# Raising weight splits, bank-emptying instructions and state updates in the order of ScalarE and VectorE

## The chip, the cores and the metric

The kernel runs on one core of a Trainium2 chip. The metric is device time in microseconds (us) of one execution; lower is better. The core has a matrix engine (TensorE, rows PE, its weight loads PEld), VectorE (DVE), ScalarE (ACT), GpSimd (POOL) and SyncE (SP), which here only issues DMA transfers. TensorE writes its results into PSUM banks, and a bank can be written anew only when VectorE or ScalarE has read it out.

## The reference, cut to what matters

One layer of a hybrid decoder: 512 prompt tokens and 64 sample tokens (8 sequences of 8) are normalised, one wide projection feeds three branches, and the branches are gated, summed and projected back. All is float32. The change touches the second branch, a Mamba-2 state-space branch (SSD) with 8 groups of 4 heads, computed in chunks of 128 tokens:

```python
xbc, conv_new = _causal_conv(xbc, conv0, conv_w, conv_b)      # 4 taps, then silu
xs, bm, cm = jnp.split(xbc, [D_INNER, D_INNER + SSD_GROUPS * SSD_STATE], axis=-1)
dt = jax.nn.softplus(dt_raw + dt_bias)
...
cb = jnp.einsum('bclgn,bcsgn->bgcls', cc, bc)
y_diag = jnp.einsum('bgcls,bgrcls,bcsgrp->bclgrp', cb, decay, xc)
states = jnp.einsum('bcsgn,bgrcs,bcsgrp->cbgrpn', bc, decay_states, xc)
h_final, h_prev = lax.scan(step, h_init, (states, chunk_decay))   # h * d + s
y_off = jnp.einsum('bclgn,cbgrpn,bgrcl->bclgrp', cc, h_prev, jnp.exp(a_cs))
...
y = y_diag + y_off + xh * d_skip[:, None]
h_b = _gated_group_rmsnorm(y.reshape(bsz, L, D_INNER), z, ssd_norm_g)   # y * silu(z), normed by group
m = g_a * (h_a @ w_proj_a) + g_b * (h_b @ w_proj_b) + g_x * (h_x @ w_proj_x)
```

## The kernel before, in words

The SSD branch is the first large stage, from about 40 to 637 us. Tokens lie along the free axis (512 + 64 = 576 columns), channels on the 128 partitions. A projection of 128 output channels is a **job** of two halves of 288 columns. Its weights come by DMA as `wraw` (two buffers, each for two jobs). `prep` splits one job's 128x1024 weights into a rounded high part `whi`, a cast on ScalarE, and a low part `wlo`, a subtraction on VectorE (both in `split`, lines 98 and 99; two buffers each). `half(f)` issues 24 matmuls (8 slices of the contraction times whi·xhi, whi·xlo, wlo·xhi, line 167) into one of three `acc` banks, and then the instructions that empty that bank.

There are four kinds of jobs. `conv_job` (four for each group) empties its bank into `raw` (lines 404, 408, 409, ScalarE) and, after the second half, runs the convolution: one scaled copy on ScalarE (line 416), three taps on VectorE (line 418), a tanh on ScalarE (line 420) and a product on VectorE (422, 426, 429); its results are `xs` and `C`. `z_job` (two for each group) empties with a tanh (462) and a product (463) into `zs`. `proj_job` multiplies the normed groups `hb` by the output projection and adds the bank to `m_sb` (753, 755). `gate_job` (eight, late) takes a tanh (732).

Between the halves stand the **steps** of the current group: transposes of a chunk (503) into an `sps` bank, from which `xdt`, `xdd` and `BT` are made (506, 509, 511); the product C·B (532) multiplied into the decays `e` (533); the diagonal part (548) added to `ysb` (559); the state matmul (567) and the state update `hT` (571, 573, 574); the off-diagonal part (592, 595, 597); for the samples the state `h` (653, 658, 659) and the stacked operands `xv`, `xst`, `bst`, `btd` (622 to 631). `gate_y` and `norm_y` norm the group before: a product, a square, two matmuls with a matrix of ones (699, 700), Ln and Exp on ScalarE (701, 702), a product (705), and a split into `hb` (again lines 98 and 99). There are three `sps` and two `yps` banks.

The order of TensorE is fixed by hand: `units` lists halves and steps, and inside `tc.manual_schedule` TensorE issues in the order in which the code emits. ScalarE and VectorE are ordered by a scheduler at build time: among the instructions that it takes to be ready, an engine gets the one with the lowest number, and the number is the place in the order of emission (TensorE's instructions count too). The result is one fixed queue for each engine; on the chip an engine takes its queue in that order and waits where an operand or a buffer isn't there. In the last loop below, the weights of job i+1 are split when the first half of job i is issued, and the loads of job i+2 are issued at the same place:

```python
i = at[id(j)]
if h == 0:
    if i + 2 < len(jobs):
        jobs[i + 2].load()
    if i + 1 < len(jobs):
        jobs[i + 1].prep()
j.half(h)
```

Of the kernel before, what the change touches and what calls it, by code (L numbers as in the profile page):

```python
# [42 lines left out]
def tile_hybrid_step(  # L43
# [33 lines left out]
    def s_tile():  # L77
# [12 lines left out]
                     compare_op=ALU.is_ge, fill=0.0, base=LS - 1, channel_multiplier=-1)  # L90


    lo_last = [False]
# [106 lines left out]
    with ExitStack() as stb:  # L200
# [177 lines left out]
        def conv_job(g, ci):  # L378
# [14 lines left out]
            def half(f):  # L393
                ps, _ = gemm_half(k["w"], KD, xh, xl, f)
                if f == 0:
                    if ci == 0:
                        d["xs"] = pb.tile([P, 3, TW], F32, tag="xs", name="xs", bufs=2)
                        d["C"] = pb.tile([P, T], F32, tag="C", name="C", bufs=2)
                        d["cg"] = pb.tile([P, 4, 27], F32, tag="cg", name="cg", bufs=2)
                    raw = k["raw"] = pb.tile([P, RAWW], F32, tag="raw", name="raw", bufs=2)  # L400
                    smp = raw[:, 515:603].rearrange("p (b t) -> p b t", t=11)
                    GP.memset(raw[:, 0:3], 0.0)
                    GP.tensor_copy(smp[:, :, 0:3], csF[:, q].rearrange("p (b k) -> p b k", k=3))
                    S.copy(raw[:, 3:3 + HT], ps)
                    return
                raw = k["raw"]
                smp = raw[:, 515:603].rearrange("p (b t) -> p b t", t=11)
                S.copy(raw[:, 3 + HT:515], ps[:, 0:TP - HT])
                S.copy(smp[:, :, 3:11], ps[:, TP - HT:HT].rearrange("p (b t) -> p b t", t=LS))

# [35 lines left out]
        def z_job(g, j):  # L446
            d = st_[g]
            k = {}

            def load():  # L450
                if j == 0:
                    d["wz"] = load_block(w_in2, 0, KD, [(O_Z + 256 * g, 256)])

            def prep():
                k["w"] = wsplit(d["wz"], KD, j * P)

            def half(f):
                if f == 0 and j == 0:
                    d["zs"] = pb.tile([P, 2, T], F32, tag="zs", name="zs", bufs=1)
                ps, sl = gemm_half(k["w"], KD, xh, xl, f)  # L460
                th = pb.tile([P, HT], F32, tag="th", name="th", bufs=2)
                S.activation(th, ps, AF.Tanh, scale=0.5)
                V.scalar_tensor_tensor(d["zs"][:, j, sl], th, 1.0, ps, ALU.add, ALU.mult)  # L463
            return Job(load, prep, half)
# [28 lines left out]
        def chunk_a(g, c):  # L493
# [11 lines left out]
            xdt = d["xdt", c] = pb.tile([P, 4, HD], F32, tag="xdt", name="xdt", bufs=3)  # L505
            V.tensor_tensor(xdt, x4, dt[:, c, h0_:h0_ + 4, None].to_broadcast([P, 4, HD]), ALU.mult)
            if not smp:
                xdd = pb.tile([P, 4, HD], F32, tag="xdd", name="xdd", bufs=2)
                V.tensor_tensor(xdd, x4, wdec[:, c, h0_:h0_ + 4, None].to_broadcast([P, 4, HD]), ALU.mult)
                BT = pb.tile([P, P], F32, tag="BT", name="BT", bufs=2)  # L510
                S.copy(BT, tp[:, 256:384])
                d["xdd", c], d["BT", c] = xdd, BT
                chunk_cb(g, c)
            else:
                stack(g, 0, tp)
# [8 lines left out]
        def chunk_cb(g, c):  # L524
            d = st_[g]
            xs, CF = d["xs"], d["C"]
            w = TS if c == 4 else P
            c0 = c * P
            e = d.pop(("ex", c))
            ew = e[:, :, 0:w]  # L530
            cb = s_tile()
            PE.matmul(cb[:, 0:w], lhsT=xs[:, 2, c0:c0 + P], rhs=CF[:, c0:c0 + w], start=True, stop=True)
            made = V.tensor_tensor(ew, ew, cb[:, None, 0:w].to_broadcast([P, 4, w]), ALU.mult)
            d["e", c] = e, d.pop(("xdt", c)), made
# [26 lines left out]
        def state(g, c):  # L561
# [7 lines left out]
            hN = d["hT", c] = pb.tile([P, 4, HD], F32, tag="hT", name="hT", bufs=2)  # L569
            if c == 0:  # L570
                S.copy(hN, s4)
            else:
                V.tensor_tensor(hN, d["hT", c - 1], dec[:, c, h0_:h0_ + 4, None].to_broadcast([P, 4, HD]), ALU.mult)
                V.tensor_tensor(hN, hN, s4, ALU.add)

# [9 lines left out]
        def y_off(g, c):  # L585
# [8 lines left out]
            t1 = pb.tile([P, 2, P], F32, tag="t1", name="t1", bufs=2)  # L594
            V.tensor_tensor(t1, yo[:, 0:256].rearrange("p (j l) -> p j l", j=2), d["ebc"][:, :, c0:c0 + P], ALU.mult)
            ys = ysb[:, :, c0:c0 + P]
# [51 lines left out]
        def h0_new(g, j, f):  # L648
# [8 lines left out]
            for b in range(4):  # L657
                S.activation(h4[:, b], h4[:, b], AF.Copy, scale=dl[:, b])
            V.tensor_tensor(h4, h4, sps.rearrange("p (b n) -> p b n", b=4), ALU.add)
            if f == 1:  # L660
# [74 lines left out]
        def proj_job(r, p):  # L735
# [10 lines left out]
            def half(j):  # L746
                jj = 2 * p + j
                w = [t[:, :, j * P:(j + 1) * P] for t in k["w"]]
                for f in range(2):
                    ps, sl = gemm_half(w, 4, lambda i: hb[4 * r + i][:, 0], lambda i: hb[4 * r + i][:, 1], f)  # L750
                    dst = m_sb[:, jj, sl]
                    if r == 0:
                        S.copy(dst, ps)
                    else:
                        V.tensor_tensor(dst, dst, ps, ALU.add)
                    if r == 3:
# [6 lines left out]
        with tc.manual_schedule(engines={mybir.EngineType.PE}):  # L763
# [68 lines left out]
            for j, h in units:  # L832
# [642 lines left out]
```

## Time and profile before

| what | value |
|---|---|
| time, median of 3 runs (lowest to highest) | 1162.23 us (1160.72 to 1164.68) |
| the profiled execution: its own time, its span | 1159.05 us, 1157.3 us |
| TensorE busy over the span | 1102.9 us, 95% |
| VectorE busy over the span | 782.0 us, 68% |
| ScalarE busy over the span | 621.9 us, 54% |
| mean granted TensorE clock | 0.991 of full speed |

The span runs from the first to the last instruction of one execution; 1.75 us of its time lie around it. Busy means that an instruction was in the engine. Matmuls follow one another in a pipeline, so a busy TensorE isn't the same as one at its peak, but an idle one is time lost if TensorE is what the end waits for. [...]

### The profile page before, as it was taken

What the parts mean: (1) busy time and instruction counts of PE and PEld (TensorE: products, weight loads), DVE (VectorE), ACT (ScalarE), POOL (GpSimd) and SP (SyncE); (2) the same over time, 40 slices, a digit from 0 to 9 for tenths busy, and PEclk for the clock granted to TensorE, in tenths of its full rate; (3) what the DMA queues carried; (4) which work ended last, traced back from release to release, by engine and by line L of the source; (5) the groups of instructions that cost most, each with busy time, mean ns of one, the idle gap of its engine ahead of it and who ended that gap; (6) DMA issues with size and microseconds to landing.
All of it is one profiled execution on the core that took longest, in us unless ns stands there. A gap on an engine that the chain in (4) does not pass through costs nothing.

```text
span 1157.3 us, 20424 instructions
## 1 busy us (share of the span) xinstructions
PE 1102.9 (95%) x8199; PEld 1024.2 (88%) x8199; DVE 782.0 (68%) x1450; ACT 621.9 (54%) x1294; POOL 37.6 (3%) x110
## 2 busy tenths in 40 slices
PE   5989999899999999989999998999999999999997
PEld 4989898899998989989999776899999999888876
DVE  5778788758787776866646545686875567665843
ACT  6457686766868476763643234344653335564521
POOL 3010010000000000100000000000000000000000
PEclk9999999999999999999999998999999999999999
DMA  6533534255443426236223423631362463455411
GB/s 188 131 80 108 155 116 136 76 151 135 118 133 115 123 87 180 72 115 172 78 78 140 139 92 122 214 110 46 101 220 101 131 186 101 122 177 181 159 47 72
DMA packets 160334, 144.90 MB, mean 125 GB/s; under 512 B 10032, under 2 KB 141136, under 8 KB 160240
## 3 DMA queue, kind: packets, MB, share of 16 engines
q1 hardware_dynamic: 137136, 126.12, 36.4%
q10 hardware_dynamic: 23104, 17.49, 4.8%
q8 instruction: 64, 1.05, 0.4%
q14 instruction: 30, 0.25, 0.1%
HBM read 124.13 MB, written 19.46 MB: 124 GB/s over the span
## 4 chain that ended last, share of the span: by engine, by line
PE 81%; DVE 7%; ACT 6%; DMA 4%; issue 2%; SPq 0%; ACTq 0%; DVEq 0%
PE acc L167 31%; PE acc L908 15%; PE acc L154 11%; PE acc L1424 4%; PE acc L1033 4%; PE yps L548 2%; DVE cacc L418 1%; DMA wraw<-in_w_in_dram 1%; PE sps L644 1%; DVE wlo L99 1%; PE sps L503 1%; ACT e L491 1%; PE sps L567 1%; PE sps L1276 1%; PE sps L592 1%
## 5 line engine op out<-in xcount | busy, mean ns | idle before, releaser
L167 PE MATMUL acc<-hn_hi,whi 128*128 128x288 f32 x896 | 272.0, 304 | 1.0 <-ACT thm L732 0.8
L167 PE MATMUL acc<-hn_hi,wlo 128*128 128x288 f32 x896 | 265.7, 297 | 3.9 <-DVE wlo L99 3.9
L167 PE MATMUL acc<-hn_lo,whi 128*128 128x288 f32 x896 | 265.3, 296 | 0.0
L167 PEld LDWEIGHTS acc<-hn_hi,wlo 128*128 128x128 f32 x896 | 169.3, 189 | 4.2 <-DVE wlo L99 4.1
L167 PEld LDWEIGHTS acc<-hn_hi,whi 128*128 128x128 f32 x896 | 169.4, 189 | 3.6 <-ACT thm L732 1.0
L167 PEld LDWEIGHTS acc<-hn_lo,whi 128*128 128x128 f32 x896 | 169.4, 189 | 0.5
L99 DVE TENSOR_TENSOR wlo<-wraw,whi 128x1024 fp32r<-128x1024 f32 x72 | 87.9, 1220 | 31.5 <-ACT whi L98 31.2
L167 PE MATMUL acc<-hb,whi 128*128 128x288 f32 x512 | 105.2, 301 | 3.1 <-DVE zs L463 2.6
L98 ACT CAST whi<-wraw 128x1024 fp32r<-128x1024 f32 x72 | 75.5, 1049 | 55.8 <-PE acc L167 48.1
L98 ACT CAST w<-wraw 128x1024 fp32r<-128x1024 f32 (+1 forms) x64 | 59.2, 941 | 79.2 <-PE acc L908 24.6
L908 PE MATMUL acc<-hn_hi,w 128*128 128x288 f32 x512 | 88.4, 300 | 0.0
L167 PEld LDWEIGHTS acc<-hb,whi 128*128 128x128 f32 x512 | 82.8, 191 | 3.5 <-DVE zs L463 2.8
L908 PE MATMUL acc<-tT,w 128*128 128x288 f32 x576 | 85.4, 298 | 0.0
L418 DVE SCALAR_TENSOR_TENSOR cacc<-raw,cwh,cacc 128x600 f32<-128x600 f32 x96 | 80.2, 837 | 4.0 <-ACT cacc L416 3.6
L99 DVE TENSOR_TENSOR w<-wraw,w 128x1024 fp32r<-128x1024 f32 (+1 forms) x64 | 68.7, 1086 | 20.1 <-ACT w L98 20.1
L908 PEld LDWEIGHTS acc<-tT,w 128*128 128x128 f32 x576 | 78.4, 188 | 0.7 <-issue 0.7
L167 PE MATMUL acc<-hb,wlo 128*128 128x288 f32 x256 | 76.1, 297 | 2.8 <-DVE wlo L99 2.8
L908 PEld LDWEIGHTS acc<-hn_hi,w 128*128 128x128 f32 x512 | 73.9, 188 | 2.1 <-issue 0.6
L491 ACT ACTIVATE e<-e,nacs 128x128 f32<-128x128 f32 (+1 forms) x160 | 50.3, 385 | 15.9 <-DVE e L489 15.8
L99 DVE TENSOR_TENSOR w<-S,w 128x1024 fp32r<-128x1024 f32 x32 | 39.1, 1223 | 25.9 <-ACT w L98 25.9
L154 PE MATMUL acc<-ha,w 128*128 128x288 f32 x384 | 51.6, 295 | 0.0
L167 PEld LDWEIGHTS acc<-hb,wlo 128*128 128x128 f32 x256 | 48.8, 191 | 3.1 <-DVE wlo L99 3.1
(392 smaller groups left out, 2143.5 us busy)
## 6 DMA issues: line engine op xcount, KB each, us to landing
wraw<-in_w_in_dram SPq DMA_DIRECT2D x44, 1024.0 KB
wraw<-in_w_in_dram SPq DMA_DIRECT2D x16, 512.0 KB
e<-a_scr SPq DMA_DIRECT2D x32, 256.0 KB
h<-in_state_ssm_dram SPq DMA_DIRECT2D x16, 512.0 KB
out_dram<-h ACTq DMA_DIRECT2D x16, 512.0 KB
wraw<-in_w_proj_b_dram SPq DMA_DIRECT2D x8, 1024.0 KB
ebc<-e_scr SPq DMA_DIRECT2D x16, 288.0 KB
wraw<-in_w_mem_kv_dram SPq DMA_DIRECT2D x4, 1024.0 KB
```

What stands on the lines that cost most here:

```text
L98: S.copy(hi, v)
L99: (e or V).tensor_tensor(lo, v, hi, ALU.subtract)
L154: PE.matmul(ps[:n, :width], lhsT=a, rhs=b[:, sl], start=(i == 0), stop=(i == last))
L167: PE.matmul(ps[:, 0:HT], lhsT=a[:, k], rhs=b(k)[:, sl], start=(n == 0), stop=(n == 3 * nk - 1))
L418: V.scalar_tensor_tensor(a[:, 0:n], raw[:, i:i + n], cwh[:, i, q:q + 1], a[:, 0:n], ALU.mult, ALU.add)
L491: S.activation(e[:, h, 0:w], e[:, h, 0:w], AF.Exp, bias=nacs[:, c, h0_ + h:h0_ + h + 1])
L503: PE.transpose(tp[:, j * P:(j + 1) * P], xs[:, j, c0:c0 + P], ident)
L548: m = PE.matmul(y4[64 * r:64 * r + 64, i, j], lhsT=xdt[:, h], rhs=e[:, h, 0:w], start=True, stop=True)
L567: PE.matmul(sps[:, 0:256], lhsT=BT, rhs=xdd.rearrange("p h d -> p (h d)"), start=True, stop=True)
L908: PE.matmul(ps[:, 0:HT], lhsT=w[:, r, k], rhs=x(q, k), start=first and n == 0, stop=n == 11, skip_group_check=True)
L1033: PE.matmul(pss[i], lhsT=x(k)[:, c], rhs=w[:, r, k2], start=(k + q == 0), stop=(k == KD - 1 and q == 2))
L1424: PE.matmul(ps[:, 0:cn], lhsT=x(k)[:, c], rhs=w, start=(k + q == 0), stop=(k == KD - 1 and q == 2))
```

## The change: a lower number in the scheduler's order

`soon(n)` is a context in which the instructions emitted get a number that is n lower than their place; after it the numbers go on as before. The scheduler then puts them in front of ready instructions that were emitted up to n places earlier. What is computed, the operands, the buffers and TensorE's order stay the same. These get it:

* by 160: all of `prep`, the splits of the next job's weights (lines 98 and 99), with no DMA in it
* by 100: the copies into `raw` (404, 408, 409), tanh and product of `z_job` (462, 463), the state update `hT` (571, 573, 574), and `m_sb` (753, 755)
* by 60: `xdt`, `xdd`, `BT` (506, 509, 511), the product into `e` (533), `t1` of `y_off` (595), and the sum into `h` (659)

These keep their place: the convolution (416 to 429), the decays (489, 491), `ysb`, the sums 559 and 597, `gate_y` and `norm_y` with the splits into `hb`, the tanh of `gate_job` (732), the scalings of `h` (658), and the stacked operands (622 to 631).

```diff
+    def soon(n):
+
+        return tc.high_priority(n)
...
-                    S.copy(raw[:, 3:3 + HT], ps)
+                    with soon(100):
+                        S.copy(raw[:, 3:3 + HT], ps)
...
-                S.copy(raw[:, 3 + HT:515], ps[:, 0:TP - HT])
-                S.copy(smp[:, :, 3:11], ps[:, TP - HT:HT].rearrange("p (b t) -> p b t", t=LS))
+                with soon(100):
+                    S.copy(raw[:, 3 + HT:515], ps[:, 0:TP - HT])
+                    S.copy(smp[:, :, 3:11], ps[:, TP - HT:HT].rearrange("p (b t) -> p b t", t=LS))
...
-                S.activation(th, ps, AF.Tanh, scale=0.5)
-                V.scalar_tensor_tensor(d["zs"][:, j, sl], th, 1.0, ps, ALU.add, ALU.mult)
+                with soon(100):
+                    S.activation(th, ps, AF.Tanh, scale=0.5)
+                    V.scalar_tensor_tensor(d["zs"][:, j, sl], th, 1.0, ps, ALU.add, ALU.mult)
...
-            V.tensor_tensor(xdt, x4, dt[:, c, h0_:h0_ + 4, None].to_broadcast([P, 4, HD]), ALU.mult)
+            with soon(60):
+                V.tensor_tensor(xdt, x4, dt[:, c, h0_:h0_ + 4, None].to_broadcast([P, 4, HD]), ALU.mult)
...
-                S.copy(BT, tp[:, 256:384])
+                with soon(60):
+                    V.tensor_tensor(xdd, x4, wdec[:, c, h0_:h0_ + 4, None].to_broadcast([P, 4, HD]), ALU.mult)
+                    S.copy(BT, tp[:, 256:384])
...
+            with soon(60):
+                made = V.tensor_tensor(ew, ew, cb[:, None, 0:w].to_broadcast([P, 4, w]), ALU.mult)
...
+            with soon(100):
+                if c == 0:
+                    S.copy(hN, s4)
+                else:
+                    V.tensor_tensor(hN, d["hT", c - 1], dec[:, c, h0_:h0_ + 4, None].to_broadcast([P, 4, HD]), ALU.mult)
+                    V.tensor_tensor(hN, hN, s4, ALU.add)
...
+            with soon(60):
+                V.tensor_tensor(h4, h4, sps.rearrange("p (b n) -> p b n", b=4), ALU.add)
...
+                    with soon(100):
+                        if r == 0:
+                            S.copy(dst, ps)
+                        else:
+                            V.tensor_tensor(dst, dst, ps, ALU.add)
...
-                        jobs[i + 1].prep()
+                        with soon(160):
+                            jobs[i + 1].prep()
```

## Rows read from the trace of the kernel before

**Rows 1.** Busy time of each engine in four stretches: the SSD stage from 60 us on, two stretches with a norm of a group in them, and one stretch behind a long wait. Columns: us, busy time (and count) of PE, PEld, DVE, ACT and POOL, granted clock, DMA share, GB/s.

```profile
60.00:637.00 577.00, 552.07 (x4435) 530.26 (x4434) 412.52 (x799) 369.85 (x866) 23.14 (x78) 0.99 0.41 118
...
340.00:360.00 20.00, 17.19 (x130) 16.69 (x129) 16.12 (x32) 18.57 (x39) 0.95 (x3) 1.00 0.14 53
480.00:500.00 20.00, 16.07 (x115) 15.56 (x114) 16.21 (x32) 19.11 (x39) 1.43 (x1) 0.96 0.10 39
...
498.30:508.00 9.70, 9.67 (x69) 9.34 (x70) 5.88 (x13) 3.74 (x10) 0.00 (x0) 0.82 0.27 62
```

**Rows 2.** What TensorE waited for in the SSD stage (60 to 637 us). Columns: waiting engine, tile and line, then the releaser: total us, times, longest us.

```profile
PE acc L167 <- DVE wlo L99: 6.7, 2, 3.9
PE sps L532 <- DVE C L422: 4.7, 1, 4.7
PE acc L167 <- DVE zs L463: 2.6, 1, 2.6
PE sps L592 <- DVE hT L574: 2.3, 4, 1.0
PE acc L699 <- DVE m_sb L755: 2.2, 1, 2.2
PE sps L503 <- DVE h L659: 2.2, 2, 1.1
PE sps L532 <- DVE hT L574: 1.1, 1, 1.1
PE acc L167 <- ACT thm L732: 0.8, 1, 0.8
PE sps L567 <- ACT BT L511: 0.6, 1, 0.6
PE sps L592 <- DVE bst L628: 0.6, 1, 0.6
PE acc L167 <- DVE m_sb L755: 0.5, 1, 0.5
```

**Rows 3.** Instructions in order of time (start us, us, engine, line) before the two waits for wlo: first ScalarE at 202 and 208 us, then VectorE at 212 to 214 us, and last the second wlo, from the chain of work that ended last.

```profile
202.16 1.28 ACT L701 ACT_TABLE_LOAD   x1
...
207.97 1.03 ACT L98 CAST whi<-wraw 128x1024 fp32r<-128x1024 f32 x1
...
212.72 0.75 DVE L99 TENSOR_TENSOR hb<-ysb,hb 128x576 fp32r<-128x576 f32 x1
...
214.26 1.23 DVE L99 TENSOR_TENSOR wlo<-wraw,whi 128x1024 fp32r<-128x1024 f32 x1
...
497.05 1.24 DVE wlo L99
```

**Rows 4.** Pieces of the chain of work that ended last (start us, us, what): matmuls of line 167 behind the two waits for wlo and a run of them in between; then the granted clock of TensorE just behind the first (us, PE busy, clock, DMA share, GB/s).

```profile
215.54 7.73 PE acc L167 x46
...
228.95 6.34 PE acc L167 x48
...
498.33 4.71 PE acc L167 x22
...
215.50:219.00 3.50, 3.46 (x16) 0.56 0.02 5
```

**Rows 5.** VectorE in order of time in front of the wait for zs.

```profile
358.08 0.84 DVE L418 SCALAR_TENSOR_TENSOR cacc<-raw,cwh,cacc 128x600 f32<-128x600 f32 x1
358.95 0.46 DVE L463 SCALAR_TENSOR_TENSOR zs<-th,acc 128x288 f32<-128x288 f32 x1
```

**Rows 6.** VectorE in order of time in front of the wait of the norm's matmul for m_sb.

```profile
416.92 0.81 DVE L755 TENSOR_TENSOR m_sb<-m_sb,acc 128x288 f32<-128x288 f32 x2
```

**Rows 7.** Pieces of the chain in front of the longest wait for hT.

```profile
493.54 0.75 DVE cacc L418
494.29 0.33 DVE hT L574
```

**Rows 8.** ScalarE in order of time before the first wait of a transpose for h.

```profile
118.05 2.44 ACT L658 ACTIVATE h<-h,ebc 128x128 f32<-128x128 f32 x8
```

**Rows 9.** VectorE in order of time before the wait for C in the first group.

```profile
64.33 1.22 DVE L99 TENSOR_TENSOR wlo<-wraw,whi 128x1024 fp32r<-128x1024 f32 x1
...
68.21 0.69 DVE L422 SCALAR_TENSOR_TENSOR C<-raw,cacc 128x512 f32<-128x512 f32 x1 [0.49 <-ACT raw L420]
```

**Rows 10.** Three of the four places where a projection of normed groups begins: VectorE's last split into hb and TensorE's first matmuls on hb, in order of time.

```profile
355.07 0.52 PE L167 MATMUL acc<-hb,whi 128*128 128x288 f32 x2
...
355.41 0.75 DVE L99 TENSOR_TENSOR hb<-ysb,hb 128x576 fp32r<-128x576 f32 x1
...
490.31 1.42 DVE L99 TENSOR_TENSOR hb<-ysb,hb 128x576 fp32r<-128x576 f32 x2
...
494.98 0.51 PE L167 MATMUL acc<-hb,whi 128*128 128x288 f32 x2
...
616.50 1.49 DVE L99 TENSOR_TENSOR hb<-ysb,hb 128x576 fp32r<-128x576 f32 x2
...
617.41 0.42 PE L167 MATMUL acc<-hb,whi 128*128 128x288 f32 x2
```

**Rows 11.** The casts to whi: how long ScalarE stood waiting for TensorE to be done with the buffer (total us, times, longest us, 60 to 637 us), and their group from 0 to 760 us (busy us, mean ns, idle before).

```profile
ACT whi L98 <- PE acc L167: 46.7, 24, 5.4
...
L98 ACT CAST whi<-wraw 128x1024 fp32r<-128x1024 f32 x72 | 75.5, 1049 | 55.8 <-PE acc L167 48.1 <-PE acc L154 3.9 <-issue 2.5
```

More of the change, by code (lines that the diff above doesn't have):

```diff
@@ L505, in chunk_a @@
             xdt = d["xdt", c] = pb.tile([P, 4, HD], F32, tag="xdt", name="xdt", bufs=3)
-            V.tensor_tensor(xdt, x4, dt[:, c, h0_:h0_ + 4, None].to_broadcast([P, 4, HD]), ALU.mult)
+            with soon(60):
+                V.tensor_tensor(xdt, x4, dt[:, c, h0_:h0_ + 4, None].to_broadcast([P, 4, HD]), ALU.mult)
             if not smp:
                 xdd = pb.tile([P, 4, HD], F32, tag="xdd", name="xdd", bufs=2)
-                V.tensor_tensor(xdd, x4, wdec[:, c, h0_:h0_ + 4, None].to_broadcast([P, 4, HD]), ALU.mult)
                 BT = pb.tile([P, P], F32, tag="BT", name="BT", bufs=2)
-                S.copy(BT, tp[:, 256:384])
+                with soon(60):
+                    V.tensor_tensor(xdd, x4, wdec[:, c, h0_:h0_ + 4, None].to_broadcast([P, 4, HD]), ALU.mult)
+                    S.copy(BT, tp[:, 256:384])
                 d["xdd", c], d["BT", c] = xdd, BT
@@ L532, in chunk_cb @@
             PE.matmul(cb[:, 0:w], lhsT=xs[:, 2, c0:c0 + P], rhs=CF[:, c0:c0 + w], start=True, stop=True)
-            made = V.tensor_tensor(ew, ew, cb[:, None, 0:w].to_broadcast([P, 4, w]), ALU.mult)
+            with soon(60):
+                made = V.tensor_tensor(ew, ew, cb[:, None, 0:w].to_broadcast([P, 4, w]), ALU.mult)
             d["e", c] = e, d.pop(("xdt", c)), made
@@ L569, in state @@
             hN = d["hT", c] = pb.tile([P, 4, HD], F32, tag="hT", name="hT", bufs=2)
[L570 to L574, printed above, removed]
+            with soon(100):
[4 more added lines that the diff above has]
+                    V.tensor_tensor(hN, hN, s4, ALU.add)
         def state_out(g):
@@ L594, in y_off @@
             t1 = pb.tile([P, 2, P], F32, tag="t1", name="t1", bufs=2)
-            V.tensor_tensor(t1, yo[:, 0:256].rearrange("p (j l) -> p j l", j=2), d["ebc"][:, :, c0:c0 + P], ALU.mult)
+            with soon(60):
+                V.tensor_tensor(t1, yo[:, 0:256].rearrange("p (j l) -> p j l", j=2), d["ebc"][:, :, c0:c0 + P], ALU.mult)
             ys = ysb[:, :, c0:c0 + P]
@@ L658, in h0_new @@
                 S.activation(h4[:, b], h4[:, b], AF.Copy, scale=dl[:, b])
-            V.tensor_tensor(h4, h4, sps.rearrange("p (b n) -> p b n", b=4), ALU.add)
+            with soon(60):
+                V.tensor_tensor(h4, h4, sps.rearrange("p (b n) -> p b n", b=4), ALU.add)
             if f == 1:
@@ L751, in half @@
                     dst = m_sb[:, jj, sl]
[L752 to L755, printed above, removed]
+                    with soon(100):
[3 more added lines that the diff above has]
+                            V.tensor_tensor(dst, dst, ps, ALU.add)
                     if r == 3:
```

## The prediction, made before the changed kernel ran

> **What bounds the kernel now.** I read the busy times of the SSD stage first. In the 577 us from 60 to 637 us TensorE is busy 552.07 us, VectorE 412.52 and ScalarE 369.85 [rows 1]. TensorE is the bound: the reader is to see that at most 577 - 552.07 = 24.9 us of idle time, and what slow matmuls behind it cost, can be won here by an order of the other engines. Second, who ended that idle time [rows 2]: the eleven waits add to 24.3 us, 20 of them for VectorE's results in the rows of wlo, C, zs, hT and m_sb alone. Third, what stood in front of each late instruction on its own engine: that decides whether a higher place helps, since the change removes no work. Fourth, whether the time comes back: in the 9.7 us from 498.3, behind a wait, VectorE is busy 5.88 of 9.70 us and ScalarE 3.74 [rows 1], so the late spots are bursts with room behind them, not engines that are full for long.
>
> **The weight splits (by 160).** Two waits for wlo take 6.7 us, the longest 3.9 [rows 2]. In the first, the cast to whi began at 207.97, behind the table loads and the Ln and Exp of a norm that began at 202.16; wlo began only at 214.26, behind a split into hb at 212.72 and others [rows 3]. All of these were emitted before it, within the last group's steps, so within 160 places or little more. The cast's buffer is free when the job before the last is done, in TensorE's order before the norm's two matmuls, so by 202.16. In front of the norm the cast takes its 1.03 us there and the subtraction 1.23 [rows 3]: wlo is ready at about 204.4 and not at 215.5. The second is alike: wlo at 497.05 [rows 3] is the last of a queue behind a norm. I take both: 6.7 us. Below: if the cast doesn't get past the norm, 0.
>
> After both waits the clock was at half: 0.56 granted over 3.5 us behind the first [rows 4], and TensorE had stood before it. In price: 46 matmuls took 7.73 us there, 48 took 6.34 later, so 46 would have taken 6.34 x 46 / 48 = 6.08 and 1.65 us were lost; 22 matmuls took 4.71 against 2.91, so 1.80 us [rows 4]. With the waits these 3.45 us go too. If a shorter wait stays in the place, they may stay; the low end is 0.
>
> **The instructions that empty acc banks (by 100).** zs 2.6, m_sb 2.2 + 0.5 [rows 2], together 5.3 us. Before the wait for zs VectorE ran a tap at 358.08 and then zs at 358.95 [rows 5]; with its number it goes in front of the taps, of 0.84 each. The two m_sb additions came back to back at 416.92 [rows 6]: the first had waited for VectorE, not for its bank. Both are then limited by their inputs. I take 5.3; low end 3, if half of it is found in the next bank.
>
> **The state update (by 100).** hT: 2.3 in four waits and 1.1 in one [rows 2]. In the last, a tap at 493.54 stood directly ahead of it at 494.29 [rows 7]. The addition itself, 0.33 us behind its matmul [rows 7], remains each time; I take 2.8 of 3.4.
>
> **The rest by 60.** BT costs 0.6 [rows 2] and I count it. The wait of a transpose for the bank that h holds, 2.2 in two [rows 2], stays: eight scalings of h take ScalarE from 118.05 to 120.49 [rows 8] and these keep their place. So do the waits for bst (0.6) and for the tanh of a gate job (0.8) [rows 2].
>
> **What is not won and what gets worse.** The wait for C in the first group, 4.7 us [rows 2], is for a convolution, which keeps its number while others rise. Between wlo at 64.33 and the product that makes C at 68.21 [rows 9] VectorE was idle for 0.49 us alone, so moving wlo ahead of the taps exchanges two pieces in one chain: between 1.2 us later (one split more in front) and 1.2 sooner. I take 1.2 later.
> The norms are pushed back too. At the second start of a projection TensorE begins on hb at 355.07, and the last split into hb runs from 355.41 to 356.16; the fourth of four slices is needed after about nine matmuls of 0.13 us (6.34 / 48, [rows 4]), at 356.2. That has no slack. The third starts at 494.98 with hb done at 491.73 and the last at 617.41 with hb done at 617.99, needed at 618.6 [rows 10]. One cast (1.05) and one bank copy in front of the norm's Exp put the second start 2.0 us late, less whatever the earlier wlo frees; I take 2.0.
> For waits that can't be read out of an order that isn't written yet I take 3.0 us, about one wait of the size of zs.
>
> No DMA moves by itself: `prep` issues none. But an earlier split frees `wraw`, so SyncE's next load can be issued some us sooner; it lands in front of its use today, since TensorE waits for no transfer [rows 2]. GpSimd's queue has only the zeroing and the copies of raw; no step is moved past them on that queue, and they depend on the convolution's end, which gets later by a split or two.
>
> **The sum.** 6.7 + 3.45 + 5.3 + 2.8 + 0.6 = 18.9 us go, 1.2 + 2.0 + 3.0 = 6.2 come: 12.7 us net, I say 13. The profiled execution took 1159.05 us, so it would become about 1146; the median of the runs lies 3.2 us above it, so the predicted median is 1162.2 - 13 = 1149.
>
> **A wait that the change adds.** ScalarE stood 46.7 us in 24 casts, waiting at the head of its queue for TensorE to be done with the buffer, 1.9 us each; the other casts of 72 mostly came late instead [rows 11]. With the casts raised more of them will be there early, and behind each stand the copies that empty banks, the tanh and the exponentials of the decays. If all of the 48 others waited 1.9 us, that would be 93 us more on an engine that has 577 - 370 - 47 = 160 idle us left [rows 1, 11], so on the whole it fits, and TensorE today loses nothing behind the 24. In the stretches at 340 and 480 us ScalarE is busy 18.57 and 19.11 of 20 us [rows 1], and there it doesn't fit. [...]
>
> **Rivals.**
> More: the wait for C goes as well, because the bank copies of the last convolution are raised and its chain starts sooner. Then 4.7 us more go, about 0.9 of slow matmuls with them, and nothing comes back: 18.9 + 5.6 = 24.5, 1138. For it: that chain begins with the bank copies. Against: VectorE's chain has no gap to close [rows 9].
> Less: the casts don't get past the norm (the scheduler counts the buffer free later than the chip does, or doesn't see the 1.28 us table loads [rows 3]). Then the bank and state terms alone remain, 5.3 + 2.8 + 0.6 = 8.7, less 3.0: 1156 to 1157.
> None: raised casts wait at the head of ScalarE's queue. In the two full stretches two casts each of 1.9 us put all behind them 3.8 us back, 7.6 us, and their two slow stretches (3.45) stay: 12.7 - 7.6 - 3.5 = 1.6 us won, 1160 to 1162.
> Slower: the norm of a group is starved. Whatever is raised goes in front of it, and hb comes d us later at each of the three starts of rows 10. The margins are 0, 4.4 (1.2 + 494.98 - 491.73) and 0.6 us, and three new waits bring three slow stretches of about 1.7: 3d - 5.0 + 5.1, so about 3d. It eats the 18.9 from d = 6.3 on; with d = 8 the sum is 24 - 18.9 = 5 us slower, 1167. For it: these starts are the tightest places, and the two norms there are already the slow stretches. Against: the raised work in such a stretch has to be done before the same point anyway, and VectorE has some 4 of 20 us idle in both [rows 1].
>
> **Chances.** Forecast 0.48, with its own range 1143 to 1154. More 0.07, less 0.16, none 0.13, slower 0.16. A measurement of this kernel can tell about 0.3%, 3.5 us, from no change. Faster: 0.48 + 0.07 + 0.15 of "less" = 0.70. Same: 0.13 + 0.01 = 0.14. Slower: 0.16. The range is 1139 to 1164: it leaves out half of "more" and most of "slower", about 0.18. Its low end lies between all gains with nothing coming back (1162.2 - 18.9 = 1143) and "more", its high end a little over no change.
>
> **What would show it.** The two rows for wlo, those for zs and m_sb and most of hT vanish from TensorE's waits; C and h stay at about 4.7 and 2.2; TensorE's idle time from 60 to 637 us falls from 24.9 to about 16 (15.4 of waits go, 6.2 come); two of the half-clock stretches go. A row of TensorE waiting for hb with more than 2 us is the step on the norms; more than 80 us of ScalarE in the casts' wait is the third rival. The prediction is wrong if TensorE's idle time stays above 21 us, or if it falls and the end of the stage doesn't come earlier.

## Result: slower by about 1.2%, and the profile after

The changed kernel took 1176.32 us (median of 4 runs, 1172.77 to 1179.5) beside 1161.47 us for the kernel before in the same comparison: a ratio of 1.0122, 95% interval 1.0089 to 1.0156. Forecast were 1149 us with a range of 1139 to 1164, and a chance of 0.16 for slower. The prediction was wrong in sign, and the time lies 12 us above its range.

The profiled execution took 1179.13 us (span 1177.4). It lies 20.1 us above the profiled one of before (1159.05 us), while the medians differ by 14.9: the profiles below are one from the upper end of its kernel's times and one from the lower end, and overstate the loss by about 5 us. First the stage of [rows 1] and what is behind it, cut at the same matmuls: the k-th matmul of one trace is the k-th of the other, and those at 60 and 637 us before stand at 63.0 and 656.35 us now (columns: busy time and count of PE, PEld, DVE, ACT, POOL, granted clock, DMA share, GB/s).

```profile
63.00:656.35 593.35, 559.97 (x4435) 536.45 (x4434) 412.98 (x799) 378.83 (x873) 23.43 (x78) 0.97 0.39 114
656.35:1177.40 521.05, 505.36 (x3429) 452.85 (x3427) 328.84 (x551) 219.59 (x362) 2.38 (x2) 0.99 0.39 129
```

The SSD stage takes 593.35 us in place of 577. TensorE's idle time in it is 593.35 - 559.97 = 33.4 us against 24.9, so 8.45 more. The other 7.9 us are in the same 4435 matmuls, busy 559.97 us against 552.07: the clock granted there fell from 0.99 to 0.97. Another 3.0 us come before the stage (63.00 against 60.00) and 0.75 after it (521.05 against 1157.30 - 637.00): 8.45 + 7.9 + 3.0 + 0.75 = 20.1, the difference of the two spans.

Second, what TensorE waited for (60 to 660 us):

```profile
PE sps L541 <- DVE bst L640: 10.4, 2, 8.4
PE sps L656 <- issue: 5.0, 2, 2.5
PE sps L541 <- DVE C L428: 5.0, 1, 5.0
PE sps L510 <- DVE h L672: 3.5, 2, 1.9
PE sps L541 <- DVE t L622: 2.5, 2, 1.7
PE sps L656 <- DVE e L543: 1.7, 1, 1.7
PE acc L171 <- DVE zs L470: 1.3, 3, 0.4
PE sps L541 <- ACT co L446: 1.1, 2, 0.6
```

The reader is to see two things. What the prediction said would go has gone: the rows for wlo, m_sb, hT behind VectorE and BT of [rows 2] are not there, and zs is down to 1.3. And every new wait above 0.7 us is one for one of the three **sps** banks (the row for C, an operand, was there with 4.7). The instructions that were to empty these banks are ones that the change left in place (`bst` 640, before 628; the samples' `t` 622, before 610; `co` 446, before 440) or raised least (`e` 543, before 533, and `h` 672, before 659, by 60).

The longest wait, 8.4 us, shows how. ScalarE's timeline of the changed kernel at the first norm, that of the first group, which is taken among the second group's steps (start, length, line, operation; here `zs` is the tile that Ln and Exp write):

```profile
155.75 1.28 ACT L714 ACT_TABLE_LOAD   x1
157.05 0.41 ACT L714 ACTIVATE zs<-acc 128x288 f32<-128x288 f32 x1
...
157.75 1.28 ACT L498 ACT_TABLE_LOAD   x1
159.05 1.07 ACT L498 ACTIVATE e<-e,nacs 128x64 f32<-128x64 f32 x4
160.12 1.28 ACT L714 ACT_TABLE_LOAD   x1
161.42 0.41 ACT L714 ACTIVATE zs<-acc 128x288 f32<-128x288 f32 x1
161.85 1.28 ACT L715 ACT_TABLE_LOAD   x1
163.14 0.68 ACT L715 ACTIVATE zs<-zs 128x576 f32<-128x576 f32 x1
```

Between the two Ln of the norm the scheduler put a group of exponentials; each change between Ln and an exponential is a table load of 1.28 us here, so Ln and Exp stretch from 155.75 to 163.82, 8.1 us. VectorE meanwhile, and TensorE:

```profile
163.86 1.54 DVE L718 SCALAR_TENSOR_TENSOR ysb<-ysb,gh,zs 128x576 f32<-128x576 f32 x2 [3.85 <-ACT zs L715]
165.32 0.74 DVE L634 TENSOR_TENSOR xv<-sps,w 96x256 f32<-96x256 f32 x2
...
166.72 1.21 DVE L103 TENSOR_TENSOR wlo<-wraw,whi 128x1024 fp32r<-128x1024 f32 x1
167.86 1.42 DVE L103 TENSOR_TENSOR hb<-ysb,hb 128x576 fp32r<-128x576 f32 x2
...
169.75 0.29 DVE L640 TENSOR_TENSOR bst<-sps,bst 32x128 fp32r<-32x128 f32 x1
...
170.09 0.69 PE L541 MATMUL sps<-C,xs 128*128 128x64 f32 x2 [8.42 <-DVE bst L640]
```

VectorE stood idle for 3.85 us with the norm's product at the head of its queue, and the stacked operands stood behind it: `xv`, which reads a bank, and `bst`, which empties it, came at 165.32 and 169.75 us. In the kernel before the norm was as good as done when VectorE reached it, and `xv` stood ahead of it:

```profile
148.86 0.41 DVE L622 TENSOR_TENSOR xv<-sps,w 96x256 f32<-96x256 f32 x1
...
154.14 1.55 DVE L705 SCALAR_TENSOR_TENSOR ysb<-ysb,gh,zs 128x576 f32<-128x576 f32 x2 [0.57 <-ACT zs L702]
155.71 0.29 DVE L628 TENSOR_TENSOR bst<-sps,bst 32x128 fp32r<-32x128 f32 x1
```

Behind the wait TensorE ran at 0.68 granted for 5.9 us: at 0.50 from 170.1 to 173 us, where the matmuls of 288 columns began 0.24 us apart, and at 1.00 from 174 to 176 us, where they began 0.13 us apart:

```profile
170.10:176.00 5.90, 5.90 (x38) 5.74 (x40) 4.91 (x11) 4.73 (x13) 0.00 (x0) 0.68 0.53 142
```

The whole program has 31 table loads against 25. Those of the stage (Ln, Exp of the norm, exponentials of the decays), busy us and mean ns of one:

```profile
L714 ACT ACT_TABLE_LOAD x13 | 16.7, 1283 | 0.2
L715 ACT ACT_TABLE_LOAD x8 | 10.3, 1283 | 0.1
L498 ACT ACT_TABLE_LOAD x4 | 5.1, 1283 | 0.1
```

In the kernel before these three counts were 10, 7 and 3; with ten loads for eight norms, some of its norms were drawn out too. Each of these loads took 1283 ns, and between the second Ln and the Exp the trace shows nothing else of that length: the load at 161.85 began 0.02 us behind the end of the Ln (161.42 + 0.41), and the Exp began 1.29 us after the start of the load.

The second kind of new wait, 2.5 us at the transposes of the initial states (656), was put down to "issue". VectorE's queue there tells more:

```profile
379.10 0.42 DVE L607 TENSOR_TENSOR t<-sps,ebc 128x256 f32<-128x256 f32 x1
379.43 1.22 DVE L103 TENSOR_TENSOR wlo<-wraw,whi 128x1024 fp32r<-128x1024 f32 x1
380.56 0.45 DVE L470 SCALAR_TENSOR_TENSOR zs<-th,acc 128x288 f32<-128x288 f32 x1
380.93 0.45 DVE L769 TENSOR_TENSOR m_sb<-m_sb,acc 128x288 f32<-128x288 f32 x1
381.29 0.84 DVE L424 SCALAR_TENSOR_TENSOR cacc<-raw,cwh,cacc 128x600 f32<-128x600 f32 x1
382.05 0.45 DVE L769 TENSOR_TENSOR m_sb<-m_sb,acc 128x288 f32<-128x288 f32 x1
382.41 0.41 DVE L543 TENSOR_TENSOR e<-e,sps 128x256 f32<-128x256 f32 x1
```

The transposes began at 382.93, just behind the product into `e`, which had been raised by 60 and stood behind a split (160), zs and two m_sb (100 each), with one tap between them. In the kernel before, `t1` and `e` of the same step stood ahead of the split and the m_sb:

```profile
360.08 0.42 DVE L595 TENSOR_TENSOR t<-sps,ebc 128x256 f32<-128x256 f32 x1
360.41 0.41 DVE L533 TENSOR_TENSOR e<-e,sps 128x256 f32<-128x256 f32 x1
...
362.18 1.22 DVE L99 TENSOR_TENSOR wlo<-wraw,whi 128x1024 fp32r<-128x1024 f32 x1
363.31 0.81 DVE L755 TENSOR_TENSOR m_sb<-m_sb,acc 128x288 f32<-128x288 f32 x2
```

In a third kind the raised split itself waits. At 470 us VectorE held its subtraction at the head of its queue for 4.85 us, until the cast was done, and the sum into `h`, for whose bank TensorE waited 1.68 us, stood behind it:

```profile
470.35 1.23 DVE L103 TENSOR_TENSOR wlo<-wraw,whi 128x1024 fp32r<-128x1024 f32 x1 [4.85 <-ACT whi L102]
...
471.85 0.68 DVE L672 TENSOR_TENSOR h<-h,sps 128x512 f32<-128x512 f32 x1
```

The samples' `t` is late in the same way at 344 us: 1.69 us for TensorE, behind a split that waited 3.37 us for its cast.

### The profile page after: what moved, and what is told of

Its sections match the earlier page's. It is cut to its first block, busy times and chain, and to the rows that moved or that the text cites. A ratio compares the mean times of both kernels' runs of the same rounds, so it can differ in the third digit from the quotient of the medians.

```text
span 1177.4 us, 20452 instructions
## 1 busy us (share of the span) xinstructions
PE 1114.6 (95%) x8199; PEld 1033.7 (88%) x8199; DVE 782.6 (66%) x1450; ACT 631.0 (54%) x1300; POOL 37.3 (3%) x110
## 4 chain that ended last, share of the span: by engine, by line
PE 81%; ACT 8%; DVE 6%; DMA 2%; issue 2%; ACTq 0%; SPq 0%; DVEq 0%
PE acc L171 32%; PE acc L923 15%; PE acc L158 12%; PE acc L1439 4%; PE acc L1048 4%; DMA wraw<-in_w_in_dram 2%; PE yps L558 1%; ACT whi L102 1%; PE sps L656 1%; ACT e L498 1%; DVE wlo L103 1%; ACT L714 1%; PE sps L510 1%; PE sps L541 1%; PE sps L577 1%
## 5 line engine op out<-in xcount | busy, mean ns | idle before, releaser
L171 PE MATMUL acc<-hn_hi,whi 128*128 128x288 f32 x896 | 275.9, 308 | 1.8 <-ACT thm L745 0.8
L171 PE MATMUL acc<-hn_hi,wlo 128*128 128x288 f32 x896 | 268.5, 300 | 0.0
L171 PE MATMUL acc<-hn_lo,whi 128*128 128x288 f32 x896 | 268.3, 299 | 0.0
L171 PEld LDWEIGHTS acc<-hn_hi,whi 128*128 128x128 f32 x896 | 172.7, 193 | 5.8 <-ACT zs L714 1.4
L171 PEld LDWEIGHTS acc<-hn_lo,whi 128*128 128x128 f32 x896 | 172.7, 193 | 0.4
L171 PEld LDWEIGHTS acc<-hn_hi,wlo 128*128 128x128 f32 x896 | 172.1, 192 | 0.1
L103 DVE TENSOR_TENSOR wlo<-wraw,whi 128x1024 fp32r<-128x1024 f32 x72 | 88.1, 1223 | 46.7 <-ACT whi L102 45.5
L102 ACT CAST w<-wraw 128x1024 fp32r<-128x1024 f32 (+1 forms) x64 | 59.2, 941 | 79.8 <-PE acc L923 24.9
L923 PE MATMUL acc<-hn_hi,w 128*128 128x288 f32 x512 | 88.3, 299 | 0.0
L158 PE MATMUL acc<-hn_hi,w 128*128 128x288 f32 x256 | 51.3, 295 | 0.0
```

The costliest lines, as they stand in the source:

```text
L102: S.copy(hi, v)
L103: (e or V).tensor_tensor(lo, v, hi, ALU.subtract)
L158: PE.matmul(ps[:n, :width], lhsT=a, rhs=b[:, sl], start=(i == 0), stop=(i == last))
L171: PE.matmul(ps[:, 0:HT], lhsT=a[:, k], rhs=b(k)[:, sl], start=(n == 0), stop=(n == 3 * nk - 1))
L923: PE.matmul(ps[:, 0:HT], lhsT=w[:, r, k], rhs=x(q, k), start=first and n == 0, stop=n == 11, skip_group_check=True)
```

## Experiments

All are compared with the kernel before on the same chip; the ratios are over that (its median was 1161.5 to 1163.8 us in the four sets). The theory that came out of the trace, **displacement**: an instruction that is raised pushes back the readers of sps banks that are raised less, and TensorE waits for them. Its rivals: the raised casts park, that is, they wait at the head of ScalarE's queue; the norm's table loads cost by themselves.

### Halves of the change

**The splits alone** (before, plus):

```diff
-                        jobs[i + 1].prep()
+                        with soon(160):
+                            jobs[i + 1].prep()
```

> The kernel before with only the weight splits raised by 160. If the loss comes from casts that stand at the head of ScalarE's queue and wait for the buffer, this one has all of it: 8 to 15 us slower than before. If it comes from raised instructions that push the unraised readers of the three sps banks back, one raised group of 2.3 us a job pushes a part of it: between 5 us faster (the 6.7 us of waits for wlo gone) and 6 slower, and waits for bst in TensorE's list.

Measured: 1173.99 us, ratio 1.0079 (1.0049 to 1.0108), 29 table loads. The largest wait of TensorE:

```profile
PE sps L596 <- ACT hb L102: 5.2, 1, 5.2
```

The name misleads. L596 is the off-diagonal part, which uses no hb; it wants an sps bank. VectorE's rows of the same moment:

```profile
159.83 0.82 DVE L709 SCALAR_TENSOR_TENSOR ysb<-ysb,gh,zs 128x576 f32<-128x576 f32 x1 [4.47 <-ACT zs L706]
...
163.24 0.29 DVE L632 TENSOR_TENSOR bst<-sps,bst 32x128 fp32r<-32x128 f32 x1
```

`bst` ended at 163.53 and TensorE went on at 163.67: the same pattern with the splits alone. The time, though, is the one that was expected of parked casts (8 to 15 us slower), not of displacement (6 at most): this run alone does not decide between them.

**All but the splits** (changed kernel):

```diff
-                        with soon(160):
-                            jobs[i + 1].prep()
+                        jobs[i + 1].prep()
```

> The change without the raised weight splits. Parked casts as the cause: no slower than before, 3 to 9 us faster, since the waits for zs, m_sb and hT go. Displaced readers of the sps banks as the cause: still slower than before by some us, waits for bst, t or e are there, and the two waits for wlo are back.

Measured: 1170.64 us, ratio 1.0062 (1.0042 to 1.0083).

```profile
PE acc L171 <- ACT whi L102: 7.6, 3, 2.6
PE sps L541 <- DVE bst L640: 7.0, 1, 7.0
PE acc L171 <- DVE wlo L103: 6.5, 3, 2.2
```

Either half is slower than before, and each displaces what the other would have raised: without the splits the wait for the weights is 14.1 us where it had been 6.7 [rows 2]. The wait for bst is there in both. That this half is slower speaks for displacement; parked casts would have made it 3 to 9 us faster.

**Only what is raised by 100** (before, plus the four edits with `soon(100)`: raw, zs, hT, m_sb):

> The kernel before with only those instructions raised that the change raises by 100 (copies into raw, tanh and product of zs, hT, m_sb). The prediction's terms for these alone: 5.3 + 2.8 = 8 us less than before, 1154 us. Theory (what is raised displaces the stacked operands and the splits, which are late already): the waits for zs, m_sb and hT go, those for wlo, whi and bst grow by as much or more, 1162 to 1172 us.

Measured: 1168.55 us, ratio 1.0047 (1.0027 to 1.0067). The waits for zs, m_sb and hT are gone, wlo stands at 9.0, bst at 4.2, whi at 3.9 and e at 3.2 us. The prediction's 8 us were taken from TensorE's list and came back elsewhere on it, as the theory expected.

### Undoing the displacement

**The stacked operands raised too** (changed kernel, plus):

```diff
-            v = pb.tile([96, 4, HD], F32, tag="t1", name="xv", bufs=2)
...
-            V.tensor_tensor(bst[64:96], tp[64:96, 256:384], bst[64:96], ALU.subtract)
+            with soon(100):
+                v = pb.tile([96, 4, HD], F32, tag="t1", name="xv", bufs=2)
...
+                V.tensor_tensor(bst[64:96], tp[64:96, 256:384], bst[64:96], ALU.subtract)
```

> The change, with the stacked operands that empty an sps bank (xv, xst, bst) raised by 100 as well. Displaced readers as the cause: the 10.4 us of waits for bst and the slow matmuls behind them go, 10 to 15 us less than the change, so about the time of before. Parked casts or table loads as the cause: within 4 us of the change.

Measured: 1160.41 us, ratio 0.998 (0.9956 to 1.0004), against 1.0122 for the changed kernel: about 16 us back, with the same 31 table loads. The wait for bst is 0.2 us. In its place the next reader in VectorE's queue behind the late norm shows, once:

```profile
PE sps L657 <- DVE t L607: 5.5, 1, 5.5
```

**Ln and Exp of the norm raised** (changed kernel, plus):

```diff
-                S.activation(rs[:, sl], ms[:, 0:HT], AF.Ln)
-            S.activation(rs, rs, AF.Exp, scale=-0.5)
+                with soon(160):
+                    S.activation(rs[:, sl], ms[:, 0:HT], AF.Ln)
+            with soon(160):
+                S.activation(rs, rs, AF.Exp, scale=-0.5)
```

> The change, with the Ln and Exp of the norm raised by 160, so that no other function comes between them: 21 table loads on ScalarE in the program and not 31. Table loads as the cause: 8 to 15 us less than the change. Displaced readers alone as the cause: the long wait for bst gets shorter by the norm's share (3 to 5 us less than the change), the waits for e, h and t stay.

Measured: 1160.82 us, ratio 0.9977 (0.9948 to 1.0005), 21 table loads. The time is the one expected of table loads; displacement alone had 3 to 5 us. The wait for bst falls to 2.5 us although the stacked operands keep their place, and a new one comes: acc banks that wait for Ln, 10.4 us in six. So the 8.4 us needed both, a reader left behind the norm and a norm drawn out by loads; the runs below test this. In both runs ScalarE's casts still waited, 52.1 us (28 casts) and 55.5 (35), against 61.6 (37) in the changed kernel, 46.7 (24) before [rows 11]: the casts still park, for 5 to 9 us longer than before, at a time that is no worse than before.

**Is the norm's order a cost by itself?** The kernel before with Ln and Exp raised by 160, nothing else:

> The kernel before, in which only Ln and Exp of the norm are raised by 160, nothing else. Theory (the drawn-out norm costs time only where other instructions have been raised into it): within 0.5% of before, 1157 to 1166 us: the wait for wlo behind the norms gets smaller by up to 4 us or larger by about 1, and waits of an acc bank for Ln come in. Rival (the norm's late Ln and its split table loads are a cost by themselves, and the rest of the change is neutral): about 16 us faster than before, 1147 us.

Measured: 1159.07 us, ratio 0.9974 (0.9955 to 0.9994). A gain of about 3 us, not 16.

**The splits and Ln** (before, plus both):

> The kernel before with the splits of the weights raised by 160, as in the first experiment, and Ln and Exp of the norm raised by 160 as well. Theory (raised casts cost by coming between Ln and Exp, which adds table loads and makes everything behind the norm late): 8 to 14 us less than the splits alone, 1160 to 1166 us, 21 table loads in place of 29. Rival (the splits displace readers on VectorE, norm or not): within 4 us of the splits alone, 1170 to 1178 us.

Measured: 1168.07 us, ratio 1.0039 (1.0023 to 1.0055), about 5 us better than the splits alone: between the 8 that the theory had at least and the 4 that its rival had at most. The waits that are left are for `t` of the off-diagonal part, 7.0 us in four, which is not raised here and in all four comes right behind a split and a product into the decays on VectorE: displacement is there without a late norm, the late norm makes it larger.

**The product into e by 160 in place of 60** (changed kernel):

```diff
-            with soon(60):
+            with soon(160):
                 made = V.tensor_tensor(ew, ew, cb[:, None, 0:w].to_broadcast([P, 4, w]), ALU.mult)
```

> The changed kernel with the product into e raised by 160 in place of 60, so that it stands no longer behind the splits of the weights, zs and m_sb. Theory (whatever reads an sps bank and is raised less than the rest is displaced): the two waits of 2.5 us at the transposes of h and the one for e of 1.7 us go, with the half-clock stretches behind them, 6 to 10 us less than the changed kernel, 1166 to 1171 us; the wait for bst (8.4 and 2.0 us) stays. Rival (these waits come from the late inputs of e, the exponentials on ScalarE between two table loads): the waits stay and the time is within 3 us of the changed kernel, 1173 to 1179 us.

Measured: 1173.96 us, ratio 1.0092 (1.0075 to 1.011). The time is the rival's, its reason isn't borne out: the waits stayed at the place but no longer for `e`. In the changed kernel a half-clock stretch lies behind only one of the three waits, the one for `e` (0.51 granted from 242.1 to 245.5 us); behind the two of 2.5 us the clock reads 1.00 (382.9 to 388 and 523.6 to 529 us).

```profile
PE sps L656 <- DVE t L607: 6.7, 3, 2.5
```

`e` and `t1` had changed places, and the one that came last behind the split and the m_sb held the bank.

**e and t1 by 160** (the edit above, and):

```diff
-            with soon(60):
+            with soon(160):
                 V.tensor_tensor(t1, yo[:, 0:256].rearrange("p (j l) -> p j l", j=2), d["ebc"][:, :, c0:c0 + P], ALU.mult)
```

> The changed kernel with the product into e and t1 of the off-diagonal part both raised by 160 in place of 60. Theory (the three waits at the transposes of h belong to whichever reader of an sps bank comes last behind a split, zs and two m_sb on VectorE): no wait over 1 us at these transposes, the two waits for bst (8.4 and 2.0 us) as in the changed kernel, 1165 to 1171 us. Rival (a third reader, the unraised bst, holds the bank then): waits of about 2 us for bst at the same transposes, 1172 to 1178 us.

Measured: 1167.96 us, ratio 1.0045 (1.0022 to 1.0067). No wait over 1 us is left at these transposes, bst stands at 10.4 us as before the edit. So this part of the loss, about 9 us by the ratios (1.0122 - 1.0045 = 0.0077), is the same displacement at a second place. It doesn't add to the 16 us of the stacked operands: together they would be more than the 14.9 that were lost.

### Do the cures add up?

**Stacked operands and Ln** (changed kernel, both edits from above):

> The changed kernel with both cures at once: the stacked operands raised by 100, and Ln and Exp of the norm raised by 160. Theory (one cost: the long waits need both an unraised reader of an sps bank and a norm that is drawn out by table loads, so that either cure alone takes the same waits away): the two together give little more than each alone, 1156 to 1161 us; no wait for bst over 1 us, 21 table loads, the wait of the acc banks for Ln (10.4 us with Ln raised alone) stays at 7 to 12 us. Rival (two costs that add up, about 16 us for the displaced readers and about 16 us for the drawn-out norm): 1144 to 1150 us.

Measured: 1157.62 us, ratio 0.9962 (0.9942 to 0.9982): faster than both kernels. The theory's time and the wait for Ln (9.3 us) are as expected: the two cures remove the same wait.

**e, t1 and the stacked operands:**

> As the run before, and the stacked operands raised by 100. Theory (the two parts of the loss are different waits and add up): 4 to 8 us less than with the stacked operands alone raised (1160.4 us against a before of 1163.1), so 1152 to 1157 us, faster than before. Rival (what is raised takes the place of something else that TensorE needs): 1159 to 1166 us, with new waits of 3 us or more for hb, h, h0T or Ln.

Measured: 1161.37 us, ratio 0.999 (0.9974 to 1.0006). No better than the stacked operands alone: the theory's sum failed here, and the time is the rival's. In the profiled execution (1157.01 us, the lowest of twelve) the wait for `t` of the samples is 0.9 us and bst is not on the list, but h holds banks for 6.3 us in three, against 3.3 with the stacked operands alone; hb shows with 2.7, as there (2.8).

**e, t1, the stacked operands and Ln:**

> As the run before, and Ln and Exp of the norm raised by 160. Against the run with the stacked operands and Ln raised (0.996 of before), in which no wait for e was left: theory: within 0.3% of it, 1154 to 1161 us, the waits for Ln of about 9 us as there. Rival: 1162 us or more, as in the run with all readers at 160.

Measured: 1154.34 us, ratio 0.993 (0.9907 to 0.9954), the best of all orders tried; that it is the best rests on six runs. Its stage, between the same matmuls as above:

```profile
61.45:630.40 568.95, 547.32 (x4435) 527.05 (x4434) 412.04 (x799) 364.19 (x863) 18.46 (x78) 1.00 0.42 119
```

Between these two single executions (1151.35 and 1159.05 us), of the 8.05 us won over the 577 of [rows 1], idle time gives 24.93 - 21.63 = 3.3, and the matmuls themselves 552.07 - 547.32 = 4.75, with a mean granted clock of 1.00. Still, TensorE's idle time is far above what the prediction hoped for (16 us).

**More readers raised.** Three runs went further: nearly every reader of an sps bank at 160, the scalings of h, co and fs among them; the same with Ln and Exp; and the stacked operands and Ln (by 220) with h's scalings and the samples' product raised. The expectation says every reader, but the copy `h0T` (658) kept its place in all three and `hT` stayed at 100. What they have in common is this (160 in the first two, 100 in the third):

```diff
-            for b in range(4):
-                S.activation(h4[:, b], h4[:, b], AF.Copy, scale=dl[:, b])
+            with soon(160):
+                for b in range(4):
+                    S.activation(h4[:, b], h4[:, b], AF.Copy, scale=dl[:, b])
```

> The changed kernel with every instruction that empties an sps bank raised by the same 160 (the products from transposes, the product into e, t1 and the samples' product, the stacked operands, scalings and sum of h, the copies co and fs); the norm stays where it is. Theory (displaced readers of the sps banks are the cost): TensorE's waits at sps banks for bst, t, e, h and co fall from 24 us to under 8, and the time to 1152 to 1158 us, below before. Rival (whatever is left unraised is displaced in its turn: the norm, hb and the taps): a new wait for hb, for wlo or for ysb of more than 5 us, and 1160 us or more.

Measured: 1165.32 us, ratio 1.0038 (1.0016 to 1.006). The waits that the theory named fell as it said (bst, t and e are off the list, h stands at 4.4 us), the time did not, and the rival's sign, a new wait of more than 5 us, isn't there either:

```profile
PE sps L669 <- DVE h L676: 3.8, 2, 2.0
...
PE sps L619 <- ACT yos L695: 3.5, 2, 2.2
PE yps L691 <- ACT h0T L662: 2.1, 4, 0.9
```

> As the run before with all readers of sps banks raised by 160, and Ln and Exp of the norm raised by 160 as well. Theory (displacement): little more than the readers alone, 1150 to 1158 us, 21 table loads in place of 27; the wait of acc banks for Ln of about 10 us costs what the fewer table loads win. Rival (the two costs add up): under 1147 us. If everything raised means that nothing is raised, the order is again like that of before: 1158 to 1163 us with the waits for wlo back.

Measured: 1161.4 us, ratio 0.9991 (0.9969 to 1.0013). The time is the third one named, without its sign: no wait for wlo came back.

> The run with the stacked operands (100) and Ln and Exp (160) raised, changed in three places: Ln and Exp by 220 so that they pass the cast of the weights, the scalings of h and its sum by 100, and the samples' product with the decays by 160. Theory (each wait left at an sps bank or for Ln is a matter of the place of its reader): the waits for Ln of 9.3 us fall by half, those for h (4.4) and t (2.9) to under 2, and the time to 1148 to 1155 us. Rival (a raised reader takes the place of another one, as in the run with all readers raised by 160): 1157 to 1166 us with new waits for hb, h0T or yos.

Measured: 1162.51 us, ratio 0.9995 (0.9977 to 1.0013); Ln's waits stayed at 9.3 us, and yos came in with 4.9. As the rival has it, what is newly late is something that was not raised: yos (3.5, 3.1 and 4.9 us in the three runs) and h0T. For yos the trace of the first run shows why. ScalarE's queue also issues transfers (rows ACTq), those of `co` among them, and yos stands behind these; at 467 us:

```profile
462.03 0.31 ACTq L451 DMA_DIRECT2D out_dram<-co  x1
465.97 0.25 ACTq L450 DMA_DIRECT2D out_dram<-co  x1
...
466.61 0.37 ACT L695 COPY yos<-yps 128x256 f32<-128x256 f32 x1 [4.34 <-DMA out_dram<-co]
```

Between two issues 3.6 us passed (465.97 - 462.34) in which ScalarE did nothing. ScalarE's idle time directly in front of yos that ended with transfers of `co` is 7.5 us in the first run and 5.3 us in the second; in the third ScalarE did not stand idle directly in front of yos (0.0 us), and its 4.9 us are not traced. What the scalings of h have to do with it, and why Ln's wait does not move with its number, was not tried.

## Why the prediction was wrong

**The terms that were to go** held. The waits for wlo (6.7), m_sb (2.7), hT behind VectorE (3.4) and BT (0.6) are gone and zs fell from 2.6 to 1.3: 6.7 + 2.7 + 3.4 + 0.6 + 1.3 = 14.7 us against the 15.4 it took out.

**The step that failed** is the paragraph on what comes back: "For waits that can't be read out of an order that isn't written yet I take 3.0 us, about one wait of the size of zs", and with it the sentence that the waits for h and "for bst (0.6)" stay because these keep their place. Keeping its place while its neighbours rise is falling back. New in the list are bst 9.8 (10.4 - 0.6), the transposes at 656 with 6.7 (5.0 + 1.7), t 2.5, h 1.3 and co 1.1: 21.4 us in place of 3.0; 21.4 + 0.3 for C - 14.7 = 7.0 us make up most of the 8.45 us of idle time, the rest is in waits under 1 us. The trace of before had the warning: bst stood with 0.6 us already on the list of [rows 2], so it was a reader without slack, and ten kinds of instructions empty the three sps banks (after the transposes of a chunk, e, the stacked operands, hT, t1, the samples' t, h, h0T, fs, co), of which the change raised some. I priced each raised instruction against what stood ahead of it and did not make the same list for what it was put ahead of. The run with the stacked operands raised gives 16 us back, and that with e and t1 about 9 us; the two overlap.

**The clock** was counted for removed waits (3.45 us) and not for new ones. The same matmuls became 7.9 us longer in the stage, nearly as much as the 8.45 of idle time.

**C and the norms.** The wait for C grew by 0.3 us, not 1.2; the projection starts had no wait for hb at all, where 2.0 us were taken.

**The rivals.** "Slower" had the sign and half of the mechanism: the norm of a group was starved, Ln to Exp lasting 8.1 us (155.75 to 163.82). But TensorE did not wait for hb, which that rival priced; it waited for unraised work that VectorE's queue had behind the norm. "None" named 80 us of casts' wait as its sign; it was 61.6, and of the two cures each won back about 16 us while this number fell by 6 to 10 us. So parked casts are not the main cause, but late casts do reach TensorE by way of VectorE, in the two waits of 1.7 us for t and h where the raised subtraction stood waiting for its cast. (That paragraph takes 72 casts, counted to 760 us, with the 24 waits of the stage to 637 us, which has 67: 43 others and not 48.) The mark that the prediction set for itself, TensorE's idle time above 21 us, was passed with 33.4.

**Still open.** A part of the raised copies into BT waits at the head of ScalarE's queue in the changed kernel (35.4 us in 21, behind xdd), and still does where the time is best but one (36.0 us in 21, stacked operands and Ln). In the best run of all it waits as long (36.7 us in 18), so it does not by itself make the kernel slower. What it costs by itself was not tried, nor what the transfers issued from ScalarE's queue cost: BT waits 15.5 us in six behind those of `co`, before 10.0 in two. Why the scheduler put the exponentials between the two Ln was not traced either. Nor was it settled whether the cure for e and t1 helps where the stacked operands are raised already: with Ln raised it reads 0.993 against 0.9962, with intervals that overlap, and without Ln 0.999 against 0.998.

## What to carry to other kernels

Before raising instructions in a scheduler's order, list for each pool of PSUM banks all instructions that empty it, with the slack of each: raising some of them moved the wait to the others here, and the reader that already showed 0.6 us of wait (bst) became the latest, with 10.4 us. Raise those together and keep a chain with changes of activation function (Ln, Exp) closed: each change between Ln and an exponential was a table load of 1.28 us here. More raising was not better here: with nearly all readers raised the time was no better than before. Look twice at a large instruction with a high rank: in the changed kernel a 1.2 us split stood ahead of the late bank reader on VectorE in each of the waits for bst, e, t and h read out above.

## What the runs showed of the hardware that was not expected

Idle time alone did not give the time. With the stacked operands raised TensorE was idle for less time in the stage than before, and yet the stage was longer by 3.9 us:

```profile
60.10:641.00 580.90, 558.05 (x4435) 534.33 (x4434) 412.58 (x799) 377.34 (x873) 21.43 (x78) 0.98 0.41 117
```

Idle are 580.90 - 558.05 = 22.85 us, 2.1 less than in [rows 1]; the same matmuls took 6.0 us longer at a granted clock of 0.98 in place of 0.99. How the waits must lie for that was not tried.

Not every slow stretch lies behind a wait of the change. From 20 to 25 us, before the SSD stage, the changed kernel's profile shows TensorE busy for all 5 us at a granted clock of 0.66, where the one before shows 1.00; a second such stretch (44 to 52 us, 0.79 against 1.00) follows. These are the 3.0 us ahead of the stage in the ledger above. The code up to 25 us is the same in every kernel here, yet one matmul at the start of the stage stands at 60.1 to 60.3 us in four of the profiled executions, at 61.1 to 61.7 in eleven and at 63.1 to 63.2 in two. So a difference of 1 to 3 us between two single executions says nothing of a change.

The column of the granted clock did not show every such stretch. In the run with e, t1, the stacked operands and Ln raised, matmuls of 288 columns follow one another at 0.24 us from 18.8 to 22.4 us, in place of 0.13 from 24 us on, as they do at a granted 0.50 in the changed kernel from 21 to 22 us, and yet the column reads 1.00 from 20 to 25 us. It reads 1.00 for the whole of 0 to 60 us too, with 328 matmuls in this run and 340 in the kernel before.
